# Issuing one tile's expert dot products and lookup table before the last tile pair, and computing one of three convolution blocks on ScalarE and GpSimd

## The chip, the cores and the metric

The kernel runs on one core of a Trainium2 chip. The metric is the device time of one execution in microseconds (us). The core's engines are named as the profile names them: PE is TensorE (PEld its weight loads), DVE is VectorE, ACT is ScalarE, POOL is GpSimd, SP is SyncE, which here issues the plain DMAs. Each engine works through its own queue of instructions in order and waits at an instruction whose inputs or buffers aren't ready.

## The reference: what is computed

One layer over 1024 tokens of width 1024, all in float32. Three parts matter here.

- **Token mixing.** A projection of the normalized input gives three groups of columns. The first (384 channels) goes through a gate and a causal depthwise convolution of width 31, then a layer norm over groups of 64 channels and a SiLU. The other two groups have a convolution of width 3 and a spatial gating. An output projection adds the result to the tokens.
- **Expert mixing.** For each token and each of 8 heads, two products with 128 keys are taken, the 16 best of each side and then the 16 best pairs: 128 experts out of 16384 per token, with softmax gates. Each chosen expert has a row of `expert_u` (dot product with the token, GELU, times the gate) and a row of `expert_v` (added with that weight).
- **Embedding gate.** A last projection, a sigmoid gate and a final normalization.

```python
y = causal_dwconv(y, conv_w) + conv_b          # width 31, 384 channels
ug = expert_u[ib]
act = jax.nn.gelu(jnp.einsum("td,tkd->tk", xb, ug)) * gb
vg = expert_v[ib]
return jnp.einsum("tk,tkd->td", act, vg)
```

## The kernel before: tiles, stages, queues

The 1024 tokens are 8 tiles of 128. The **front** works in four pairs of tiles, (0,1), (2,3), (4,5), (6,7), called the first to the fourth pair here. Each pair goes through `mix_in` (projection, convolutions, norms), `mix_out` (output projection) and `choose` (key products, the best 16, `select`).

In `mix_in` the convolution of width 31 has three blocks of 128 channels, j = 0, 1, 2, each with an accumulator `cacc` of 128x256 (128 channels by 256 tokens of the pair). Line 174 starts it on ACT. Lines 177 to 180 add 30 more taps to each block: 90 DVE instructions per pair, 360 in all, one every tap, each reading the shifted input `ya` and `cacc` and writing `cacc`. Lines 239 to 252 then norm each block; they take scratch tiles from the pool under the name `csq`, of which there are two.

The experts are done in two ways. Tiles 5, 6, 7 (`GATHER`) fetch the rows of each chosen expert by indirect DMA, which POOL issues (lines 536 and 566), and DVE forms the dot product (line 538) and the sum (line 568). Tiles 1 to 4 (`DENSE`) multiply with all 16384 experts on PE, with a weight table that holds the gate of each chosen expert and zero elsewhere. Tile 0 (`MIXED`) takes the dot products by gather and the second half by table.

A table is built by `gate_table` (lines 395 to 434): PE transposes gates and keys, ACT copies them to `gT`, `eT` and `mT`, of which there is one buffer each. Then 32 quads follow, each of four tokens: DVE compares the first key with a row of numbers (line 415), POOL does the second key in every other quad (line 421, four instructions), ACT in the remaining ones (lines 426 and 427), or DVE for the MIXED tile (line 423); PE multiplies (line 430), ACT copies out (line 431). Every eight quads SP stores the piece `st` to `Wd` (line 434). For the MIXED tile the gate is the finished weight `wm` (lines 541 to 547), so its table needs all 128 dot products per token, in four blocks of 32 (`u_step`).

Tables are issued by a **filler** list: `fill` (line 319) advances the first generator of the list by three steps at eight places in `mix_out` and eight in `choose`. Tables join the list after their pair's `choose`. The lines at the end of the front set it:

```python
    for t0, nt in ((0, 2), (2, 2), (4, 2), (6, 2)):
        yT = mix_in(t0, nt)
        choose(t0, nt, mix_out(t0, nt, yT))
        if t0 == UAT:
            for b in range(P // KB):
                u_step(MIXED, b, True)
        filler.extend(gate_table(t0 + t) for t in range(nt) if t0 + t in DENSE)
        if t0 == GAT:
            filler.append(gate_table(MIXED))
    while filler:
        fill()
```

With `UAT = GAT = 6` the MIXED tile's dot products and its table are written after the fourth pair. Then comes one block of dot products of tile 5 (line 640), and the front's buffers are released.

The order of the text isn't the order of the queues: the program is handed to a planner (`schedule_with_timeline_sim=True`, line 732) that simulates the engines and puts each instruction into its queue when it finds it ready, taking the one written earlier first. In an engine's queue the order is then fixed.

The front's gathers have three buffers `g`; the stage after it has five, in other space. That **dense stage** (lines 436 to 519) streams all experts: three products per matrix on PE (lines 481 to 483 and 504 to 506), splits on ACT and POOL (lines 468 to 477). Its buffers lie where the front's lay, and it needs every table. The gathers of tiles 5 to 7 (`experts`, line 550) run beside it. The **back** (lines 676 to 692) does the embedding gate of each tile.

Of the kernel before, what the change touches and what calls it, by code (L numbers as in the profile page):

```python
# [8 lines left out]
F32 = mybir.dt.float32  # L9
# [4 lines left out]
AF = mybir.ActivationFunctionType  # L14
OP = mybir.AluOpType
AX = mybir.AxisListType
P = 128
# [9 lines left out]
def trunk(ctx: ExitStack, tc: tile.TileContext, x, pT, w_inF, w_inV, chan, ln_c, w_sT, b_s, w_out, g_row,  # L27
          w_q, skT, expert_u, expert_uT, expert_v, w_pe, w_pg, out):
    nc = tc.nc
# [18 lines left out]
    ch = const.tile([P, chan.shape[1]], F32, name="ch")  # L48
# [7 lines left out]

    UAT, GAT, RATE = 6, 6, 3

    FG, BG = 3, 5

# [16 lines left out]
    work = fctx.enter_context(tc.tile_pool(name="work", bufs=2))  # L79
# [59 lines left out]
    def mix_in(t0, nt):  # L139

        T = nt * P
# [20 lines left out]
        yas, accs = [], []  # L162
# [13 lines left out]
            accs.append(acc)  # L176
        for k in range(1, 31):
            for j in range(3):
                nc.vector.scalar_tensor_tensor(accs[j], yas[j][:, k:k + T], ch[:, j * 31 + k:j * 31 + k + 1],
                                               accs[j], op0=OP.mult, op1=OP.add)  # L180


        for j in range(2):
# [3 lines left out]
            m = work.tile([P, 2 + T], F32, name="mb")  # L187
# [5 lines left out]
            for k in range(1, 3):  # L193
                nc.vector.scalar_tensor_tensor(acc, m[:, k:k + T], conv_b_w[:, j * 3 + k:j * 3 + k + 1], acc,
                                               op0=OP.mult, op1=OP.add)
# [432 lines left out]
# [9 lines that stand above are left out]
# [99 lines left out]
```

## Time and profile before

| | us |
|---|---|
| median of 3 runs (2860.47 to 2866.61) | 2861.89 |
| the profiled execution, its own time | 2862.61 |
| its span, first to last instruction | 2860.8 |
| PE busy (92% of the span) | 2620.5 |
| DVE busy (75%) | 2156.9 |
| POOL busy (68%) | 1945.5 |
| ACT busy (35%) | 1007.6 |

The mean granted PE clock of the profiled execution is 0.955 of full speed. Shares over the whole span mix the three stages, so the rows further down are taken stage by stage. A row's "idle" time is that of the engine just before the named instructions, with the instruction that ended it.

### The profile page before, as it was taken

To read this page: it belongs to the slowest core of one execution; us is meant where nothing else is said; L and a number is where in the kernel's file an instruction comes from. 1 tells how busy PE (TensorE), PEld (TensorE's weight loads), DVE (VectorE), ACT (ScalarE), POOL (GpSimd) and SP (SyncE) were. 2 spreads that over 40 slices of the span, in tenths; PEclk is the share of its full clock that TensorE was granted. 3 is DMA by queue.
4 is the path that set the end of the run, shared out by engine and by line. 5 is a ranking of instruction groups with operands and counts; after the bars stand their busy time and mean duration, and the time that the engine had idled before them with its cause. 6 is when DMAs were issued, how large, how long until landed. Compare 5 with 4: busy or idle time off the path is not lost.

```text
span 2860.8 us, 37645 instructions
## 1 busy us (share of the span) xinstructions
PE 2620.5 (92%) x12671; PEld 2203.2 (77%) x12671; DVE 2156.9 (75%) x4738; ACT 1007.6 (35%) x1930; POOL 1945.5 (68%) x1740
## 2 busy tenths in 40 slices
PE   7998999889678678999999999999999999999988
PEld 6887888688677656888787888878787788788767
DVE  5567888999977886777777777777777777677776
ACT  3312455335764544222322223232222322222342
POOL 0000377347876787888878888888887878888773
PEclk9998999899789779999999999999999999999999
DMA  6353688787657649899999999999999999999885
GB/s 203 129 185 120 236 300 301 242 304 253 221 206 274 228 184 339 317 324 344 331 333 328 331 347 330 338 329 342 325 336 329 328 348 332 335 339 324 299 290 174
DMA packets 299698, 820.92 MB, mean 287 GB/s; under 512 B 26096, under 2 KB 117616, under 8 KB 296944
## 3 DMA queue, kind: packets, MB, share of 16 engines
q0 software_dynamic: 129024, 469.82, 45.8%
q1 hardware_dynamic: 170480, 348.70, 35.6%
q8 instruction: 100, 1.64, 0.2%
q14 instruction: 94, 0.77, 0.1%
HBM read 764.93 MB, written 53.48 MB: 286 GB/s over the span
## 4 chain that ended last, share of the span: by engine, by line
PE 33%; DMA 23%; DVE 17%; POOL 13%; issue 10%; ACT 2%; SPq 0%; POOLq 0%; DVEq 0%; ACTq 0%
DMA g<-expert_u,idx 10%; DMA g<-expert_v,idx 10%; PE z L158 4%; DVE g L538 4%; POOL g L536 4%; PE mm L612 3%; POOL vl L477 3%; PE mm L504 3%; PE z L481 3%; PE z L482 3%; PE mm L505 3%; PE mm L506 3%; PE z L483 3%; PE mm L299 2%; PE mm L267 2%
## 5 line engine op out<-in xcount | busy, mean ns | idle before, releaser
L536 POOL DMA_INDIRECT g<-expert_u,idx x512 | 511.9, 1000 | 369.6 <-DVE g L538 163.2
L568 DVE SCALAR_TENSOR_TENSOR accP<-g,act,accP 128x1024 f32<-128x1024 f32 x384 | 493.2, 1284 | 210.9 <-DMA g<-expert_v,idx 207.4
L538 DVE SCALAR_TENSOR_TENSOR g<-g,nP 128x1024 f32<-128x1024 f32 x352 | 422.8, 1215 | 178.5 <-DMA g<-expert_u,idx 177.1
L566 POOL DMA_INDIRECT g<-expert_v,idx x384 | 367.7, 957 | 144.4 <-DVE accP L568 60.7
L504 PE MATMUL mm<-vh,ah 128*128 128x512 f32 x1024 | 400.3, 392 | 13.5 <-DVE accA L508 6.8
L481 PE MATMUL z<-nh,uh 128*128 128x512 f32 x1024 | 401.8, 393 | 8.1 <-DVE al L490 5.9
L482 PE MATMUL z<-nl,uh 128*128 128x512 f32 x1024 | 400.6, 391 | 2.0 <-DVE nl L446 2.0
L483 PE MATMUL z<-nh,ul 128*128 128x512 f32 x1024 | 400.2, 391 | 0.0
L505 PE MATMUL mm<-vl,ah 128*128 128x512 f32 x1024 | 399.2, 391 | 0.0
L506 PE MATMUL mm<-vh,al 128*128 128x512 f32 x1024 | 396.7, 390 | 0.0
L421 POOL TENSOR_SCALAR oh<-iota,eT,gT 128x128 f32<-128x128 f32 x320 | 314.5, 991 | 63.9 <-PE gt L430 50.8
L468 ACT CAST uh<-u 128x1024 fp32r<-128x1024 f32 x128 | 134.8, 1053 | 574.8 <-PE z L482 459.3
L477 POOL TENSOR_TENSOR vl<-v,vh 128x512 fp32r<-128x512 f32 x256 | 328.2, 1302 | 3.2 <-ACT vh L475 0.7
L470 POOL TENSOR_TENSOR ul<-u,uh 128x1024 fp32r<-128x1024 f32 x128 | 309.3, 2417 | 6.9 <-ACT uh L468 4.6
L430 PE MATMUL gt<-oh,oh 128*128 128x128 f32 x1280 | 221.4, 321 | 95.1 <-POOL oh L421 40.4
L430 PEld LDWEIGHTS gt<-oh,oh 128*128 128x128 f32 x1280 | 194.5, 224 | 123.1 <-POOL oh L421 82.6
L475 ACT CAST vh<-v 128x512 fp32r<-128x512 f32 x256 | 153.1, 621 | 306.9 <-DMA v<-expert_v 250.6
L538 DVE SCALAR_TENSOR_TENSOR g<-g,hrow 128x1024 f32<-128x1024 f32 x160 | 197.3, 1236 | 72.3 <-DMA g<-expert_u,idx 72.2
L158 PE MATMUL z<-aT,w 128*128 128x256 f32 x960 | 227.0, 393 | 16.0 <-DMA w<-w_inF 13.1
L299 PE MATMUL mm<-nT,w 128*128 128x256 f32 x1024 | 237.0, 383 | 4.4 <-DMA w<-w_q 4.4
L508 DVE TENSOR_TENSOR accA<-mm,accA 128x512 f32<-128x512 f32 x320 | 217.8, 684 | 27.0 <-PE mm L506 26.7
L504 PEld LDWEIGHTS mm<-vh,ah 128*128 128x128 f32 x1024 | 193.0, 189 | 56.7 <-DVE accA L508 9.8
(368 smaller groups left out, 4586.6 us busy)
## 6 DMA issues: line engine op xcount, KB each, us to landing
u<-expert_uT SPq DMA_DIRECT2D x128, 512.0 KB, 6.4
v<-expert_v SPq DMA_DIRECT2D x128, 512.0 KB, 4.9
Wd<-st SPq DMA_DIRECT2D x20, 2048.0 KB, 8.4
w<-w_q SPq DMA_DIRECT2D x64, 512.0 KB, 4.8
w<-Wd SPq DMA_DIRECT2D x128, 256.0 KB, 9.7
w<-w_inF SPq DMA_DIRECT2D x60, 512.0 KB, 3.6
wo<-w_out SPq DMA_DIRECT2D x32, 512.0 KB, 4.5
g<-expert_u,idx POOLq DMA_INDIRECT x512, 6.3
```

What stands on the lines that cost most here:

```text
L430: nc.tensor.matmul(pw[:, :, k], oh2[:, k], oh1[:, k], start=True, stop=True)
L477: nc.gpsimd.tensor_tensor(vl, v[:, s * 512:s * 512 + 512], vh.bitcast(F32), op=OP.subtract)
L481: nc.tensor.matmul(ph, uh[:, c], nh[:, c], start=c == 0, stop=False)
L482: nc.tensor.matmul(ph, uh[:, c], nl[:, c], start=False, stop=False)
L483: nc.tensor.matmul(ph, ul[:, c], nh[:, c], start=False, stop=c == 7)
L504: nc.tensor.matmul(po, ah[:, c], vh, start=i == 0, stop=False)
L505: nc.tensor.matmul(po, ah[:, c], vl, start=False, stop=False)
L506: nc.tensor.matmul(po, al[:, c], vh, start=False, stop=i == NG - 1)
L536: nc.gpsimd.indirect_dma_start(out=ug, out_offset=None, in_=expert_u, in_offset=bass.IndirectOffsetOnAxis(ap=idx[:, k:k + 1], axis=0))
L538: nc.vector.scalar_tensor_tensor(ug, ug, 1.0, ns[t, front], op0=OP.mult, op1=OP.mult, accum_out=dots[:, k - b * KB:k - b * KB + 1])
L566: nc.gpsimd.indirect_dma_start(out=vg, out_offset=None, in_=expert_v, in_offset=bass.IndirectOffsetOnAxis(ap=idx[:, kk:kk + 1], axis=0))
L568: nc.vector.scalar_tensor_tensor(acc, vg, act[:, k:k + 1], acc, op0=OP.mult, op1=OP.add)
```

## The change

Two edits, nothing else differs.

- `UAT` and `GAT` go from 6 to 4: the MIXED tile's four blocks of dot products are written behind the third pair, and its table joins the filler list behind that of tile 4, so that the list is worked off within the fourth pair's `mix_out` and `choose`.
- Of the three convolution blocks, block j = 2 loses its 30 DVE instructions per pair. In their place ACT multiplies the tap by its weight into a new scratch tile `csq` (the two that the norm uses too), and POOL adds it to `cacc`.

```diff
-    UAT, GAT, RATE = 6, 6, 3
+    UAT, GAT, RATE = 4, 4, 3
...
         for k in range(1, 31):
             for j in range(3):
-                nc.vector.scalar_tensor_tensor(accs[j], yas[j][:, k:k + T], ch[:, j * 31 + k:j * 31 + k + 1],
-                                               accs[j], op0=OP.mult, op1=OP.add)
+                tap, w = yas[j][:, k:k + T], ch[:, j * 31 + k:j * 31 + k + 1]
+                if j == 2:
+
+                    m = work.tile([P, T], F32, name="csq")
+                    nc.scalar.activation(m, tap, AF.Copy, scale=w)
+                    nc.gpsimd.tensor_tensor(accs[j], accs[j], m, op=OP.add)
+                else:
+                    nc.vector.scalar_tensor_tensor(accs[j], tap, w, accs[j], op0=OP.mult, op1=OP.add)
```

## Rows read from the trace of the kernel before

**Rows 1.** Stages: length; PE, PEld, DVE, ACT, POOL busy; clock; DMA share; GB/s.
```profile
0.00:286.00 286.00, 247.20 (x1386) 214.66 (x1386) 178.88 (x661) 82.49 (x183) 13.44 (x21) 0.97 0.48 159
286.00:787.00 501.00, 435.70 (x2589) 388.31 (x2590) 452.86 (x1531) 241.81 (x553) 294.29 (x273) 0.92 0.76 265
787.00:1042.00 255.00, 192.94 (x1067) 171.89 (x1065) 206.18 (x752) 152.03 (x358) 186.06 (x183) 0.81 0.60 217
1042.00:1085.00 43.00, 30.42 (x176) 25.51 (x176) 28.35 (x67) 13.36 (x25) 38.67 (x49) 0.87 0.69 263
1085.00:2727.00 1642.00, 1598.88 (x6948) 1309.29 (x6949) 1195.21 (x1632) 474.00 (x742) 1337.44 (x1130) 0.99 0.94 332
2727.00:2861.00 134.00, 115.41 (x510) 93.54 (x508) 95.44 (x100) 43.94 (x75) 75.61 (x87) 0.94 0.65 223
```

**Rows 2.** By line: count, ns min/median/max, first and last start in us.
```profile
L481 PE MATMUL z<-nh,uh x1024: 387/389/632, 1086.5 to 2689.2; 128*128 128x512 f32 x171
...
L508 DVE TENSOR_TENSOR accA<-mm,accA x320: 677/683/693, 1139.0 to 2727.5; 128x512 f32<-128x512 f32 x160
...
L571 ACT COPY hrow<-accP x3: 1016/1017/1017, 1702.3 to 2830.2; 128x1024 f32<-128x1024 f32 x3
```

**Rows 3.** By line, in the same columns: what ends just before the dense stage.
```profile
L434 SPq DMA_DIRECT2D Wd<-st x3: 319/319/320, 1059.3 to 1084.9; - x3
...
L530 ACT ACTIVATE nP<-hrow,rB x1: 1123/1123/1123, 1084.8 to 1084.8; 128x1024 f32<-128x1024 f32 x1
```

**Rows 4.** Timeline of PE: start us, us; the transposes that open the five tables.
```profile
304.06 0.27 PE L401 MATMUL gt<-ident,gate 128*128 128x128 f32 x1
...
627.00 0.27 PE L403 MATMUL gt<-ident,e 128*128 128x128 f32 x1
...
764.80 0.42 PE L401 MATMUL gt<-ident,gate 128*128 128x128 f32 x1
...
893.06 0.27 PE L401 MATMUL gt<-ident,gate 128*128 128x128 f32 x1
...
1016.52 0.42 PE L401 MATMUL gt<-ident,wm 128*128 128x128 f32 x1
```

**Rows 5.** Stretches between the tables, in the columns of the first group.
```profile
486.00:622.00 136.00, 116.17 (x665) 100.27 (x665) 122.14 (x416) 40.09 (x75) 45.59 (x44) 0.89 0.80 278
622.00:1016.00 394.00, 310.18 (x1779) 277.83 (x1778) 337.30 (x1260) 240.72 (x575) 292.90 (x275) 0.85 0.66 231
```

**Rows 6.** POOL's groups from 622 to 1085 us: busy, mean ns, idle before.
```profile
L421 POOL TENSOR_SCALAR oh<-iota,eT,gT 128x128 f32<-128x128 f32 x256 | 247.2, 975 | 58.8 <-PE gt L430 46.3 <-ACT eT L407 11.0
L536 POOL DMA_INDIRECT g<-expert_u,idx x79 | 91.1, 1153 | 55.2 <-DVE g L538 31.4 <-issue 5.0 <-DVE ti L334 4.2
```

**Rows 7.** The convolution on DVE: line 179 in 0 to 286, 286 to 787, 486 to 622, 622 to 1085 us.
```profile
L179 DVE SCALAR_TENSOR_TENSOR cacc<-ya,ch,cacc x180: 468/479/486, 31.5 to 182.1; 128x256 f32<-128x256 f32 x180
...
L179 DVE SCALAR_TENSOR_TENSOR cacc<-ya,ch,cacc x180: 455/472/718, 303.9 to 719.2; 128x256 f32<-128x256 f32 x180
...
L179 DVE SCALAR_TENSOR_TENSOR cacc<-ya,ch,cacc 128x256 f32<-128x256 f32 x48 | 21.7, 473 | 0.0
...
L179 DVE SCALAR_TENSOR_TENSOR cacc<-ya,ch,cacc 128x256 f32<-128x256 f32 x42 | 19.5, 475 | 0.0
```

**Rows 8.** The front's dot products and the MIXED tile's weights, by line.
```profile
L538 DVE SCALAR_TENSOR_TENSOR g<-g,hrow x160: 1154/1215/3060, 319.6 to 978.4; 128x1024 f32<-128x1024 f32 x160
...
L547 POOL TENSOR_TENSOR wm<-wm,gate x4: 269/402/602, 441.8 to 826.4; 128x32 f32<-128x32 f32 x4
```

**Rows 9.** Nearest prices: an ACT product, two POOL two-input operations, POOL's table instruction alone.
```profile
L192 ACT ACTIVATE bacc<-mb,ch x8: 503/504/507, 53.5 to 602.3; 128x256 f32<-128x256 f32 x8
...
L477 POOL TENSOR_TENSOR vl<-v,vh 128x512 fp32r<-128x512 f32 x256 | 328.2, 1302 | 3.2 <-ACT vh L475 0.7
...
L470 POOL TENSOR_TENSOR ul<-u,uh 128x1024 fp32r<-128x1024 f32 x126 | 303.6, 2410 | 6.9 <-ACT uh L468 4.6
...
L421 POOL TENSOR_SCALAR oh<-iota,eT,gT x64: 781/791/1460, 1018.6 to 1083.0; 128x128 f32<-128x128 f32 x64
```

## Prediction

> **What bounds the kernel now.** I read the stages first, because shares of the whole span mix three different limits. The busy time by stage [rows 1] cuts the run at 1085 us and 2727 us. From 1085 to 2727 the dense stage has PE busy 1599 of 1642 us at clock 0.99, with DMA at 0.94: nothing in the change touches its work, so it only starts sooner or later. Beside it run the gathers of tiles 5 to 7; dense ends with the last sum at 2727.5, the gathers with the copy at 2830.2 [rows 2]. Both begin with the same event, so a front that ends X earlier moves both by X, and the back with them.
>
> What ends the front? Just before PE's first dense product at 1086.5 [rows 2] stand the last store of a table piece at 1084.9 and, at 1084.8, the scaling of the token row from which the gather stage forms its dot products [rows 3]. Both wait for the MIXED tile's table. So I looked for what sets that table's end. The transposes that open the tables start at 304, 627, 765, 893 and 1016.5 us [rows 4]: the MIXED table is the last of a chain of four that runs without a gap from 627 to 1085, one behind the other since `gT`, `eT` and `mT` have one buffer. Its weights were ready at 826.4 [rows 8], so it waited 190 us for its turn and not for its inputs.
>
> What paces the chain? Tables 2, 3 and 4 took 138, 128 and 123 us (differences of the starts), the MIXED table, nearly alone, 69. From 622 to 1016 DVE is busy 337 of 394 us (86%), PE 79%, POOL 74% [rows 5]. POOL's queue shows why they couple: its 79 gathers there wait 31 us for DVE to free a gather buffer, and its table instructions 46 us for PE [rows 6]; behind a waiting gather stands the next quad. From 486 to 622 DVE is at 90% and POOL at 34% [rows 5]: no table runs there, as tile 2's choice isn't out of DVE yet. DVE is the engine nearest to full from 286 on (453 of 501 us, [rows 1]).
>
> **Part one, the convolution block: what DVE loses.** 360 instructions become 240. Of the 120 removed, 60 belong to the first two pairs (180 instructions end by 182 us, [rows 7]), where DVE is busy 179 of 286 us and PE 247 [rows 1]: worth nothing, PE sets the pace. The other 60 belong to the third and fourth pair. Their spacing is 0.46 us (19.5/42, 21.7/48, [rows 7]), so 60 x 0.46 = 27.6 us. Only 42 of those 180 lie behind 622 us, so 14 of the removed 60, 6.4 us, lie in the table chain and 46, 21.2 us, before it.
>
> What does the freed time before 622 do? The MIXED tile's dot products fill it: though written behind the fourth pair they run from 319.6 us on [rows 8], wherever DVE has room. One takes about 1.22 us of DVE (1.215 median), so some 17 of them move out of the chain's stretch, and 17 gathers with them. The chain's DVE load falls by 21.2 + 6.4 = 27.6 us, its POOL load by 17 x 1.153 = 20 us [rows 6]. With DVE pacing the chain, it ends 27.6 us earlier. Bounds: 0, if PE and POOL pace it, and 27.6/0.86 = 32 us, if DVE keeps its share. I take 27.6, one us for one.
>
> **What ACT and POOL gain.** 120 ACT products at 0.504 us [rows 9]: 60 us, 30 of them from 286 to 787 where ACT is busy 242 of 501 [rows 1]. Hidden; with no cover, 30 us. 120 POOL adds of 128x256: no such row, but 512 columns take 1.302 us and 1024 take 2.410 [rows 9], so 2.16 ns a column and 1.302 - 256 x 0.00216 = 0.75 us. Beside a busy DVE the table instruction takes 0.975 instead of 0.791 us on average [rows 6, 9], a factor 1.23, so 0.92 us. Bounds: 0.75 unstretched, and 1.4 at that instruction's longest over its median (1.460/0.791, [rows 9]). I take the mean stretch, 0.92. The first 60 meet a POOL that is busy 13 of 286 us [rows 1]. The third pair's 30 lie beside table 1, which has slack until table 2 starts at 627. Of the fourth pair's 30, about 14 fall behind 622: 14 x 0.92 = 13 us (20 at the upper bound), no more than the 20 us of gathers that leave. So POOL's load in the chain falls by 7 us; taken as nothing.
>
> The new waits: an ACT product needs one of two `csq` tiles and so the add two taps back. Behind a held product in ACT's queue stand the copies out of PSUM (lines 301, 308, 431), for which PE waits. I cost that at nothing in this sum, as POOL has 66% idle before 622, and price it in the second rival.
>
> **Part two, the move.** Nothing is added or removed. The 128 gathers, their 128 dot products, the row load, the four GELUs and gate products go ahead of the fourth pair in the planner's order. As they already fill gaps from 319.6 us on, only those left when the fourth pair's work is ready change place; the weights come earlier, where 190 us are spare. The table's 64 POOL instructions, 96 DVE and 128 PE instructions and four stores go ahead of most of the fourth pair's `choose`. On SP the key and query weights of `choose` then queue behind stores that wait for their piece; 16 of the 20 stores stand among such loads now, so I cost this at nothing. But the chain stays a chain: behind tile 4's table the MIXED one can't start sooner than now, and ahead of it the two only change places. I take 0. The other end is the stretch in which nothing but this table is left, 1042 to 1085: 43 us [rows 1], if it all went beside other work.
>
> **Sum.** Against the profiled execution's 2862.6 us (span 2860.8): 2862.6 - 27.6 - 0 = 2835.0. That execution stands 0.7 above the median shown, so 2834. What is late next: the same chain, 28 us earlier.
>
> **The rivals.** First, slower: **the adds stop DVE.** In place of the removed instruction POOL reads `cacc` and the product while DVE works on blocks 0 and 1, each of its instructions with two inputs from SBUF. If an add holds DVE for its length, 60 adds x 0.75 = 45 us in the third and fourth pair, against 27.6 saved: +17, so 2880. It decides from 27.6/0.75 = 37 holding adds on. For it: table instructions on POOL stretch from 0.791 to 0.975 us beside DVE, and a convolution step took up to 0.718 us with POOL busy, at most 0.486 with POOL idle [rows 6, 7, 9]. Against it: the median step is 0.472 us with POOL busy and 0.479 without [rows 7]. Held products on ACT would work the same way and sign. 0.25.
>
> The Trainium skill has a rule for this (SBUF — State Buffer, "Who interferes with whom"): a DVE instruction with two SBUF inputs and a GpSimd instruction that reads SBUF exclude each other for the whole instruction. By that rule the sum would be the 2880 of this rival; the trace agrees for POOL's stretch and hardly for DVE, whose median doesn't move, and no row has a two-input POOL operation beside the convolution.
>
> Second, **no change**: DVE's freed time only brings the MIXED weights sooner, which have 190 us spare, and the chain goes at the pace of PE and POOL (46 us of waits between them, [rows 6]); the planner leaves the table last. 2862. For it: POOL's 74% with waits both ways. Against: DVE at 86%. 0.13.
>
> Third, **both parts pay**: the MIXED table really goes beside the fourth pair's choice, and the 43 us fall away too: 2862.6 - 27.6 - 43 = 2792. Against it: DVE, PE and POOL are each at 73 to 81% from 787 to 1042 [rows 1], so there is little room for 69 us of coupled work. 0.10.
>
> **The numbers.** The forecast has 0.52; its own range is 2812 to 2854. A measurement of this kernel can tell 0.2%, 5.7 us, from no change. Faster: 0.52 + 0.10 = 0.62; same 0.13; slower 0.25. Cases of both signs are needed for 8 in 10: the range goes from the third rival's 2792 to the first's 2880.
>
> **What would show it.** Right: line 179 has 240 instructions of 0.47 us; the second table opens 15 to 25 us before 627; the MIXED table is still the last, right behind tile 4's, and opens near 990; the first dense product comes near 1058; the length from there to the end stays 1774 us. Wrong: convolution steps or dot products on DVE that lengthen, or ACT products that wait for POOL (first rival); table starts that don't move (second); a MIXED table that ends before the last choice is out of DVE, with PE going straight from choice to dense (third). A dense stage that itself changes length would be none of these.

## The result and the profile after

The changed kernel is slower: 2906.3 us median against 2861.2 for the kernel before on the same chip, ratio 1.0151 (95% interval 1.0128 to 1.0174). The profiled execution took 2905.06 us (2862.61 before), so 42.5 us more. The forecast was 2834.

First the stages of the changed kernel, by busy time in stretches; the columns are those of [rows 1], and the cuts are the same up to 1085 us.

```profile
0.00:286.00 286.00, 248.93 (x1366) 215.15 (x1366) 154.40 (x541) 100.29 (x223) 64.27 (x80) 0.96 0.47 158
286.00:787.00 501.00, 423.26 (x2439) 373.27 (x2438) 427.74 (x1354) 250.04 (x574) 322.81 (x311) 0.90 0.72 252
787.00:1042.00 255.00, 187.84 (x1123) 171.92 (x1124) 200.92 (x761) 160.00 (x377) 178.58 (x181) 0.84 0.65 229
...
1127.00:2762.00 1635.00, 1593.61 (x6924) 1302.19 (x6925) 1195.78 (x1630) 467.53 (x729) 1333.83 (x1124) 0.99 0.94 332
```

The dense stage, to its last sum at 2762, has its work and nearly its length (1635 against 1642 us), only later. In the front, from 286 to 787, POOL is busy 29 us more and ACT 8 us; DVE (428 against 453) and PE (423 against 436) are less busy: the front is slower although the two engines with the most to do got emptier.

Next, by line: the two ends of the front that answer to [rows 2] and [rows 3], and PE's transposes that open tables 2 to 5, which answer to [rows 4].

```profile
L440 SPq DMA_DIRECT2D Wd<-st x3: 320/320/326, 1089.4 to 1125.7; - x3
...
L487 PEld LDWEIGHTS z<-nh,uh x1024: 186/188/334, 1127.3 to 2731.6; 128*128 128x128 f32 x171
...
L577 ACT COPY hrow<-accP x3: 1017/1018/1019, 1745.0 to 2870.0; 128x1024 f32<-128x1024 f32 x3
```
```profile
645.55 0.33 PE L409 MATMUL gt<-ident,e 128*128 128x128 f32 x1 [1.28 <-DVE e L384]
...
794.23 0.27 PE L407 MATMUL gt<-ident,gate 128*128 128x128 f32 x1
...
921.87 0.27 PE L407 MATMUL gt<-ident,gate 128*128 128x128 f32 x1
...
1049.46 0.42 PE L407 MATMUL gt<-ident,wm 128*128 128x128 f32 x1
```

The last table store comes at 1125.7 us instead of 1084.9, the dense stage starts right behind it, and the last copy of the gather stage comes at 2870.0 instead of 2830.2. From the first dense instruction to the end of the span it is 1776 us, 1774 before. So all of the loss arises in the front, as all of the gain was meant to. The second table opens at 645.6 instead of 627.0, the third at 794 instead of 765, the fourth at 922 instead of 893, the last at 1049.5 instead of 1016.5. So 19 us of the loss build up before the chain of tables and 11 in its first link, none in the second; the last 12 us come behind the fourth table's opening, where no convolution runs any more, and what makes these isn't shown.

The convolution's three instructions, by line (count, ns min/median/max, first and last start), and ACT's waits:

```profile
L184 POOL TENSOR_TENSOR cacc<-cacc,csq x120: 712/738/6079, 46.7 to 669.2; 128x256 f32<-128x256 f32 x120
...
L186 DVE SCALAR_TENSOR_TENSOR cacc<-ya,ch,cacc x240: 459/480/1536, 32.1 to 721.6; 128x256 f32<-128x256 f32 x120
...
L183 ACT ACTIVATE csq<-ya,ch x120: 491/508/535, 46.1 to 666.7; 128x256 f32<-128x256 f32 x120
its engine sat idle before it (us, times) until:
  POOL cacc L184: 81.3, 74
```

DVE's convolution steps, at most 718 ns before [rows 7], now take up to 1536; ACT's products wait 81 us for POOL's adds. Both are signs that the prediction had listed for its first rival. An add takes 0.74 us in the median and 6.08 at the longest; that longest one is taken up below.

### The profile page after: what moved, and what is told of

Read it like the earlier page. It is cut to its first block, busy times and chain, and to the rows that moved or that the text cites. A ratio compares the mean times of both kernels' runs of the same rounds, so it can differ in the third digit from the quotient of the medians.

```text
span 2903.3 us, 37904 instructions
## 1 busy us (share of the span) xinstructions
PE 2630.7 (91%) x12671; PEld 2208.0 (76%) x12671; DVE 2146.7 (74%) x4618; ACT 1063.2 (37%) x2053; POOL 2043.2 (70%) x1860
## 4 chain that ended last, share of the span: by engine, by line
PE 34%; DMA 19%; DVE 18%; POOL 14%; issue 11%; ACT 2%; POOLq 0%; SPq 0%; DVEq 0%; ACTq 0%
DMA g<-expert_u,idx 9%; DMA g<-expert_v,idx 8%; POOL g L542 4%; DVE g L544 4%; PE mm L510 4%; PE mm L511 4%; PE mm L512 4%; PE z L487 4%; PE z L488 4%; PE z L489 3%; PE mm L618 3%; DVE accP L574 3%; POOL oh L427 3%; POOL vl L483 3%; PE z L158 2%
## 5 line engine op out<-in xcount | busy, mean ns | idle before, releaser
L158 PE MATMUL z<-aT,w 128*128 128x256 f32 x960 | 234.5, 402 | 23.7 <-DVE mb L195 10.3
L487 PEld LDWEIGHTS z<-nh,uh 128*128 128x128 f32 x1024 | 193.8, 189 | 56.1 <-DVE al L496 10.9
```

The lines of the kernel that those rows point to most:

```text
L487: nc.tensor.matmul(ph, uh[:, c], nh[:, c], start=c == 0, stop=False)
```

## The experiments

All ratios are to the kernel before on the same chip. "DVE" is DVE's busy time in the profiled execution; before it is 2156.9 us. Runs e5 to e7, e9, e13 to e16 and e18 leave out or replace part of the convolution, as their text says.

| run | ratio | 95% interval | DVE, us |
|---|---|---|---|
| the change | 1.0151 | 1.0128 to 1.0174 | 2146.7 |
| e1 the move alone | 1.0030 | 1.0012 to 1.0048 | 2159.8 |
| e2 the convolution edit alone | 1.0169 | 1.0144 to 1.0194 | 2150.5 |
| e3 e2 with four product tiles | 1.0135 | 1.0113 to 1.0156 | 2150.4 |
| e4 e2 in the first two pairs | 1.0051 | 1.0029 to 1.0073 | 2147.5 |
| e12 e2 in the last two pairs | 1.0122 | 1.0107 to 1.0138 | 2167.1 |
| e5 products, no adds | 0.9976 | 0.9960 to 0.9992 | 2111.9 |
| e6 adds, no products | 1.0157 | 1.0123 to 1.0191 | 2154.3 |
| e7 neither | 0.9991 | 0.9972 to 1.0010 | 2113.6 |
| e8 blocks in another order | 1.0000 | 0.9985 to 1.0015 | 2157.2 |
| e9 two fills for each add | 1.0065 | 1.0041 to 1.0089 | 2113.0 |
| e14 three fills | 1.0027 | 1.0011 to 1.0043 | 2114.4 |
| e13 three fills, last two pairs | 1.0001 | 0.9985 to 1.0017 | 2138.1 |
| e15 one-input POOL instruction | 1.0072 | 1.0044 to 1.0099 | 2120.4 |
| e16 adds on block 0, no products | 1.0023 | 1.0004 to 1.0041 | 2145.9 |
| e18 adds on block 1, no products | 1.0085 | 1.0066 to 1.0104 | 2157.9 |
| e17 e2 on block 0 | 1.0102 | 1.0079 to 1.0125 | 2147.0 |
| e10 table quads from POOL to DVE | 0.9986 | 0.9970 to 1.0003 | 2205.5 |
| e11 e2 and e10 | 1.0168 | 1.0141 to 1.0194 | 2191.4 |

### Which edit, and which pairs

```diff
# e1
-    UAT, GAT, RATE = 6, 6, 3
+    UAT, GAT, RATE = 4, 4, 3
# e2: the second hunk of the change without the first; in e4 and e12 its condition is
-                if j == 2:
+                if j == 2 and t0 < 4:
# (t0 >= 4 in e12)
```

> Only the MIXED tile's dot products and table are moved (UAT = GAT = 4); the convolution stays on DVE. Theory H (ACT products that wait for POOL's adds hold ACT's queue): no loss, 2855 to 2870 us. Theory M (the dot products, now ahead of the fourth pair, delay its mixing on DVE): most of the 45 us, above 2885.

> Only the convolution's third block goes to ACT and POOL; UAT = GAT = 6 as before. H and theory P (the adds fill POOL's queue and so slow the tables and gathers): most of the loss, 2890 to 2915. M: about 2861. The forecast's reason (DVE is relieved): 2835.

The move alone costs 0.3%, hardly more than can be told from nothing. In its profiled execution tables 2 to 5 open at 623.3, 771.4, 898.8 and 1015.9 us and the dense stage starts at 1087.1, 0.6 us from where it did: the front's length is the same, so the move's 0 stands where the prediction placed it. That execution is the fastest of the ten, 11 us under their median, so it doesn't show where the 0.3% lie. The convolution edit alone is as slow as the whole change.

> The convolution edit in the first two pairs alone, where POOL has hardly any other work; 60 of the 120 adds. H and P: a small loss, from the first two mixes ending 5 to 10 us later, 2862 to 2872. If a mere change of the planner's order is what costs: any value, as large as with all four pairs.

> The convolution part of the change in the third and fourth pairs alone; the first two pairs as before. With the first two pairs alone the ratio was 1.0051, with all four 1.0169: if the two halves simply add, 1.010 to 1.014 here. The first mix ends at 110 us as before.

The two halves add: 0.51% and 1.22% make 1.73%, measured 1.69%. A third of the loss comes from the first two pairs, which the prediction held to be worth nothing.

### Which instruction of the edit

```diff
# e3, against e2: four tiles in turn instead of two
-                    m = work.tile([P, T], F32, name="csq")
+                    m = work.tile([P, T], F32, name="csq" if k % 2 else "xc")
# e5, against e2: the adds left out
-                    nc.gpsimd.tensor_tensor(accs[j], accs[j], m, op=OP.add)
# e6, against e2: the tap itself is added, unscaled, with no product on ACT
-                    m = work.tile([P, T], F32, name="csq")
-                    nc.scalar.activation(m, tap, AF.Copy, scale=w)
-                    nc.gpsimd.tensor_tensor(accs[j], accs[j], m, op=OP.add)
+                    nc.gpsimd.tensor_tensor(accs[j], accs[j], tap, op=OP.add)
# e7, against e6: block 2 keeps its first tap alone
-                    nc.gpsimd.tensor_tensor(accs[j], accs[j], tap, op=OP.add)
+                    pass
# e8, against the kernel before
-            for j in range(3):
+            for j in (2, 1, 0):
```

> As the convolution alone, but the products alternate between the tiles csq and xc, so that four buffers stand between ACT and POOL instead of two. H: at least half of the convolution's loss comes back and ACT's waits for the adds (81 us in the changed kernel) fall below 40. P: no more than a quarter of the loss comes back, as the adds are the same.

> UAT = GAT = 6. Block j = 2 keeps its 120 ACT products, and the 120 POOL adds are left out, so this block's convolution is incomplete. Theory H (products that wait for POOL's adds, one queue holding the other): the loss is gone, at or below the kernel before, ratio 0.985 to 1.002. Theory A (ACT's own 60 us of products are the cost): ratio 1.010 or more. Theory P (POOL's adds as work): ratio 0.985 to 1.002.

> UAT = GAT = 6. Block j = 2 has the 120 POOL adds, of the unscaled input, and no ACT products, so its convolution is unweighted. H: ratio 0.985 to 1.004, as no ACT instruction waits for POOL in the convolution. P: most of the loss stays, 1.010 to 1.017. A: 0.985 to 1.002.

> UAT = GAT = 6. Block j = 2 keeps only its first tap: 120 DVE instructions are gone and nothing stands in their place. The forecast's own term: 27.6 us less, ratio 0.990. If DVE's freed time is only filled by other waits: 0.998 to 1.002. If a mere change of the planner's order costs tens of us: above 1.005.

> The kernel before with the three blocks' taps written in the order 2, 1, 0 in place of 0, 1, 2: the same instructions, another tie for the planner. If the result hangs on how the planner happens to fall: a ratio off 1 by more than 0.005. Under H and P: 0.998 to 1.002.

Two things follow. **The forecast's own term isn't there.** e7 has 120 fewer DVE instructions and nothing in their place; DVE is busy 43 us less (2156.9 to 2113.6), and the time stays the same within 0.3%. **The adds carry the loss.** With them and without products it is 1.57%; with products and without them there is none (0.24% less time). So products held behind adds aren't needed for the loss. Four tiles cut ACT's waits from 84 to 63 us, not below 40 as held products would have it, and gave back a fifth, so e3 by itself decides little. The other order of e8 is as fast as the first.

What the adds do to DVE shows in the last column of the table: e6 has the DVE instructions of e7 and is busy 40.7 us longer, 0.34 us for each of 120 adds.

### The adds or POOL's time

An add could hurt in two ways: P, POOL and DVE shut each other out; or Q, POOL's queue is simply longer, so that gathers and table quads come later. Fills write the same accumulator and read nothing.

```diff
# e9, against e6; e14 has range(3); e13 has range(3) and "if j == 2 and t0 >= 4"
-                    nc.gpsimd.tensor_tensor(accs[j], accs[j], tap, op=OP.add)
+                    for _ in range(2):
+                        nc.gpsimd.memset(accs[j], 0.0)
# e15, against e6
-                    nc.gpsimd.tensor_tensor(accs[j], accs[j], tap, op=OP.add)
+                    nc.gpsimd.tensor_scalar(accs[j][:, 0:P], accs[j][:, 0:P], w, w, op0=OP.mult, op1=OP.add)
```

> Block 2 of the convolution keeps only its first tap (that part of the computation is left out), and each of its 120 steps gives POOL two fills of the 128x256 accumulator, which write SBUF and read none of it. One fill of 128x128 took 0.20 us at the start of the kernel before, so some 0.7 us for a step, beside 0.80 us for an add without a product: POOL's queue is as full as with the adds. Theory P (an add on POOL and a DVE instruction with both inputs in SBUF shut each other out, and the loss is DVE's): DVE's convolution instructions stay under 0.5 us, the first mix ends at 110 us as before, the ratio lies within 0.997 to 1.002. Theory Q (POOL's time itself: gathers and one-hots queue behind the adds): the first mix ends at 110 us too, since POOL has nothing else to do there, but the second table opens at 640 to 655 us instead of 629, and the ratio is 1.008 to 1.013.

> As the run with two fills for each of block 2's 120 steps in all four pairs (block 2 keeps only its first tap), with three: 360 fills of 0.31 us are 113 us of POOL, more than the 96 us of the adds without products. Theory P (the loss is DVE and POOL shutting each other out): 0.997 to 1.004, so that the 1.0065 of the two fills was the order in which the planner laid out that program. Theory Q (POOL's time itself): half as much again as with two, 1.009 to 1.013.

> Each of block 2's 120 steps is one POOL instruction with a single SBUF tensor as input, a 128x128 half of the accumulator times a tap plus a tap (block 2's convolution is replaced by this). The one-hots of that form and size take 0.79 us when alone, so 95 us of POOL, as much as the adds. If reading SBUF on POOL at all shuts out DVE's instructions with two SBUF inputs: 17 convolution instructions ahead of the first mb take 10 us or more (6.8 with fills, 12.7 with adds), first mix at 114 to 119 us, ratio 1.008 to 1.018. If it takes two inputs on POOL as well: 6.8 us, first mix at 110, ratio 0.998 to 1.005.

The first pair shows the mechanism by itself, since POOL has no gathers and no table there. Below are the timelines (start, us, instruction, count, idle time) of DVE and POOL in e6, with adds: 17 convolution steps, the product `mb` for which PE waits, and POOL's run beside them.

```profile
46.28 12.69 DVE L184 SCALAR_TENSOR_TENSOR cacc<-ya,ch,cacc 128x256 f32<-128x256 f32 x17
58.89 0.41 DVE L193 TENSOR_TENSOR mb<-z,sg 128x256 f32<-128x256 f32 x1
...
73.22 0.42 DVE L193 TENSOR_TENSOR mb<-z,sg 128x256 f32<-128x256 f32 x1 [0.55 <-ACT sg L190]
...
47.19 24.67 POOL L182 TENSOR_TENSOR cacc<-cacc,ya 128x256 f32<-128x256 f32 x30 [15.35 <-DVE cacc L184]
```

The same in e14, with three fills for each add; DVE's queue has the same 17 steps there:

```profile
46.12 6.81 DVE L185 SCALAR_TENSOR_TENSOR cacc<-ya,ch,cacc 128x256 f32<-128x256 f32 x17
52.92 0.42 DVE L194 TENSOR_TENSOR mb<-z,sg 128x256 f32<-128x256 f32 x1
...
63.42 0.42 DVE L194 TENSOR_TENSOR mb<-z,sg 128x256 f32<-128x256 f32 x1 [1.43 <-ACT sg L191]
...
47.01 30.91 POOL L183 MEMSET cacc<- 128x256 f32 x84 [15.45 <-ACT cacc L174]
```

And in e15, with one SBUF tensor as POOL's input:

```profile
44.48 6.81 DVE L184 SCALAR_TENSOR_TENSOR cacc<-ya,ch,cacc 128x256 f32<-128x256 f32 x17
51.20 0.42 DVE L193 TENSOR_TENSOR mb<-z,sg 128x256 f32<-128x256 f32 x1
...
45.42 23.83 POOL L182 TENSOR_SCALAR cacc<-cacc,ch 128x128 f32<-128x128 f32 x30 [15.06 <-ACT cacc L174]
...
45.42 6.19 POOL L182 TENSOR_SCALAR cacc<-cacc,ch 128x128 f32<-128x128 f32 x1 [15.06 <-ACT cacc L174]
```

The last line is the first of the thirty by itself.

Seventeen steps take 12.69 us beside adds (0.75 each) and 6.81 (0.40 each) beside fills, with POOL busy throughout in both. e15's 6.81 has another reason: there DVE shut POOL out, as the times say. POOL's first instruction started inside the seventeen steps, took 6.19 us and ended 0.3 us behind the last of them; the median of all 120 is 0.45. It isn't the price of the first instruction of its kind either: the first of the kernel before (line 421) takes 2.15 us. So e15 doesn't show that POOL instructions with one SBUF input leave DVE alone; it shows the other side of the same exclusion.

`mb`, one of whose inputs is in PSUM, takes 0.41 to 0.42 us in all three. PE can't go on without `mb`: over the run its projections (line 158 in all these kernels) wait 12.6 us for it in e6, 10.3 in the change and not at all in e14. The second `mb` starts at 73.2 us with adds and at 63.4 with fills. In the kernel before it starts at 63.3, so fewer steps ahead of it bring nothing: with fills DVE sits idle 1.43 us before it, for ACT. That is how relief can be worth nothing and delay its full length. The first pair ends 10 us late in the change (last SiLU at 119.4 us instead of 109.6), 9 us in e6 (118.3), and 1 to 2 us in e14 and e15 (111.2 and 110.8), as in e7 (111.0), which has nothing in place of the steps.

The change itself comes to its 10 us by a longer way than e6. This is its first pair, first POOL, then DVE, then ACT, and DVE's next eleven steps:

```profile
46.71 6.08 POOL L184 TENSOR_TENSOR cacc<-cacc,csq 128x256 f32<-128x256 f32 x1 [15.43 <-ACT csq L183]
...
45.39 6.81 DVE L186 SCALAR_TENSOR_TENSOR cacc<-ya,ch,cacc 128x256 f32<-128x256 f32 x17
56.84 0.42 DVE L195 TENSOR_TENSOR mb<-z,sg 128x256 f32<-128x256 f32 x1 [4.63 <-ACT sg L192]
...
52.82 0.51 ACT L183 ACTIVATE csq<-ya,ch 128x256 f32<-128x256 f32 x1 [5.79 <-POOL cacc L184]
...
62.49 8.30 DVE L186 SCALAR_TENSOR_TENSOR cacc<-ya,ch,cacc 128x256 f32<-128x256 f32 x11
```

Here the seventeen steps keep their 0.40 us and the first add is the one that waits: it takes 6.08 us and ends 0.6 us behind the last step. ACT's third product waits 5.79 us for it, the copy `sg`, which `mb` needs, stands in ACT's queue behind products, and DVE sits idle 4.63 us. Only then do adds and steps alternate, and the next eleven steps take 8.30 us (0.75 each; 5.68 for the same eleven in e14). In e6 the first add, in the same place, took 0.85 us and slowed DVE from there on. The 6.08 aren't a cost of the first add as such: in e3 and e4, with the same products, it took 0.94 and 0.93 us, and e4, where adds and steps alternate from the start, ends the first pair just as late (last SiLU at 119.4 us). So POOL and DVE shut each other out in both, but the one that waits differs, and in the change a part of the delay reaches DVE through ACT. How the loss of the change divides between these two ways, no run shows.

For the third and fourth pair e12 and e13 are the comparison: adds, with their products on ACT, and fills of the same POOL time.

> In the third and fourth pairs block 2 keeps only its first tap (that part is left out) and each step gives POOL three fills of the accumulator instead of an add: 180 fills of 0.31 us are 56 us of POOL, as much as the 56 us that the 60 adds of these pairs took in the changed kernel, and none of it reads SBUF. Theory Q (in these pairs POOL's time itself is the cost): 21 us for the 38 us of fills of the run before make 32 us for 56, ratio 1.009 to 1.013, the same as with the adds within 0.3%. Theory P (the shutting out is the cost here as in the first pair): the fills cost 1.002 to 1.007, well under the adds.

Busy time by stretch, in the columns of [rows 1], then two DVE groups from 340 to 650 us (count, busy, mean ns, idle before). With adds (e12):

```profile
340.00:490.00 150.00, 128.21 (x724) 111.49 (x724) 120.90 (x325) 83.74 (x217) 132.38 (x126) 0.92 0.75 268
490.00:650.00 160.00, 131.24 (x746) 115.26 (x744) 142.95 (x444) 61.46 (x126) 84.09 (x81) 0.90 0.74 258
...
L544 DVE SCALAR_TENSOR_TENSOR g<-g,hrow 128x1024 f32<-128x1024 f32 x73 | 94.5, 1296 | 23.8 <-DMA g<-expert_u,idx 23.7
L186 DVE SCALAR_TENSOR_TENSOR cacc<-ya,ch,cacc 128x256 f32<-128x256 f32 x74 | 46.9, 649 | 0.1
```

With fills (e13):

```profile
340.00:490.00 150.00, 130.50 (x765) 114.48 (x764) 114.40 (x334) 79.55 (x208) 129.24 (x185) 0.95 0.78 274
490.00:650.00 160.00, 144.98 (x859) 128.90 (x858) 144.43 (x511) 55.77 (x112) 95.31 (x156) 0.96 0.85 293
...
L543 DVE SCALAR_TENSOR_TENSOR g<-g,hrow 128x1024 f32<-128x1024 f32 x80 | 98.3, 1231 | 39.5 <-DMA g<-expert_u,idx 39.3
L185 DVE SCALAR_TENSOR_TENSOR cacc<-ya,ch,cacc 128x256 f32<-128x256 f32 x84 | 39.1, 480 | 0.1
```

POOL is as full from 340 to 490 in both (132 and 129 us). DVE's steps take 0.65 us with adds and 0.48 with fills, the dot products 1.30 and 1.23; from 490 to 650 DVE is as busy with adds for 67 instructions fewer, and PE gets 14 us less done (at a granted clock of 0.90 instead of 0.96). DVE's busy time over the run differs by 29 us, the times by 1.2%, 34.6 us. e6 and e14 compare the same without products, over all four pairs: POOL is busy 2050.0 and 2061.0 us, DVE 2154.3 and 2114.4, and the losses are 1.57 and 0.27%. Nor is it the wait for the last POOL instruction of a block: in the third pair the last fill of e14 ends at 520 us and the last add of e6 at 481, and yet the pair's last SiLU starts at 558 in e14 and at 579 in e6. So POOL's time as such (Q) isn't the cost here; what adds and DVE's steps do to each other (P) is. That the longer steps are what makes these two pairs late is argued from these rows; only the first pair shows it step by step.

One part doesn't fit. Fills in all pairs cost 0.65% with two and 0.27% with three, and e15 0.72%, with at most 2 us of delay in the first pair and 0, 1 and 7 us more of DVE's busy time than e7. More POOL time costing less isn't Q. These programs also differ in the order into which the planner put the queues, and that may move a run by about half a per cent; no run shows this by itself (e8's other order cost nothing).

### Where the adds stand, and a lighter POOL

```diff
# e16 (against e6: adds of unscaled taps) and e17 (against e2); e18 is e16 with j == 1
-                if j == 2:
+                if j == 0:
# e10 (against the kernel before) and e11 (against e2): POOL builds every fourth quad, DVE the next odd one
-                    if n_gt[0] % 2:
+                    if n_gt[0] % 4 == 1:
...
-                    elif t == MIXED:
+                    elif n_gt[0] % 2 or t == MIXED:
```

> The adds without products on block 0 instead of block 2 (block 0's taps are added unscaled), so that the planner lays out another order with the same adds. If the loss is the adds' own, whatever the order: first mix 6 to 10 us late, ratio 1.012 to 1.018. If it was one unlucky order: 0.998 to 1.008.

> Adds without products on block 1, whose samples are ready between those of block 0 (1.0023) and block 2 (1.0157). If the place in the pair sets the cost: between the two, 1.005 to 1.012, first mix at 116 to 119 us. If it is the luck of each order: anywhere from 1.000 to 1.016, with no relation to the place.

> The convolution part of the change, whole, on block 0 in place of block 2. Block 0's samples are ready first, so the adds run earlier in each pair. If the place of the adds is what costs, as the 1.0023 of adds without products on block 0 says: 0.999 to 1.006, and better than the change itself by at least 1%. If the adds cost the same wherever they stand, and the run on block 0 was one lucky order: 1.012 to 1.018.

The same 120 adds cost 0.23, 0.85 and 1.57% on blocks 0, 1 and 2, though DVE's busy time rises by 32, 44 and 41 us over e7. The first pair ends 6 us late in e16 and 8 in e18 (last SiLU at 116.0 and 118.0 us); for e16 that is as much as the whole loss (0.23%, 6.6 us). In the third pair the adds stand in POOL's timeline like this in e16, on block 0:

```profile
307.86 11.91 POOL L182 TENSOR_TENSOR cacc<-cacc,ya 128x256 f32<-128x256 f32 x13 [7.30 <-ACT cacc L174]
322.43 1.37 POOL L540 DMA_INDIRECT g<-expert_u,idx  x1 [2.66 <-DVE idx L396]
...
326.93 6.66 POOL L182 TENSOR_TENSOR cacc<-cacc,ya 128x256 f32<-128x256 f32 x5
333.74 1.90 POOL L540 DMA_INDIRECT g<-expert_u,idx  x1
```

Thirteen run before the first gather of the pair. In e6, on block 2, the first of them starts at 361.9 us and the 30th at 480. So the loss goes with the place in the pair, in the order that e18's expectation gave. But the whole change on block 0 came out at 1.0102, not at the 0.999 to 1.006 expected of it: there the products add 0.8%, on block 2 they added nothing. Place and laid-out order can't be told apart further with these runs.

> The kernel before with every second of POOL's groups of four one-hots (40 groups) built on DVE, in the way that the MIXED tile's already are (128x128, 0.40 us each on DVE against 0.98 us on POOL): POOL gives up 157 us between 345 and 1085 us and DVE takes 64 us. Theory Q (POOL's queue sets the pace of the third and fourth pairs): tables open earlier from the second on, the last table store comes 15 to 40 us earlier, ratio 0.985 to 0.995. Theory P (DVE sets the pace, and the adds hurt by slowing it): DVE's further 64 us come on top, ratio 1.005 to 1.02.

> The convolution part of the change (products on ACT, adds on POOL) together with the half of POOL's one-hot groups moved to DVE. POOL gets about 96 us of adds and gives up 157 us. Theory Q: most of the loss of the convolution part (ratio 1.017 alone) goes, ratio 0.990 to 1.003, and what stays is the first pair's 9 us. Theory P: DVE has more to do beside the same adds, ratio 1.017 or more.

Both theories were wrong on e10. DVE got 49 us more to do and POOL 146 us less (1799.3 against 1945.5 busy), and the time moved by 0.14%, with no change inside the interval. It isn't DVE's load as such, then: 49 us more cost nothing here, in the tables and with POOL relieved at the same places, and 41 us cost 1.57% in e6, where they fall on the convolution. That the place makes this difference is argued, not shown. Together with e7, no relief of either engine by itself shortens the front; this is the nearest to a version that beats the kernel before, beside e5, which computes less. With the adds beside it (e11) the loss is whole again, though POOL has less to do than before: one more sign against Q.

## Why the prediction was wrong

- **The step that failed** is "With DVE pacing the chain, it ends 27.6 us earlier". e7 takes those instructions away, DVE is busy 43 us less, and the time shows 0 (0.9991), the lower bound that the text named ("0, if PE and POOL pace it"). DVE's high share was read as a limit; e10 shows that 49 us more on DVE, with POOL lighter, cost nothing either.
- **The second failed term** is POOL's load "taken as nothing". It was reckoned as POOL's busy time only. The add itself was sized well: 0.92 us foretold, 0.90 on average in the change (107.8/120). e13 confirms the rest of that part: POOL time without reads costs nothing in these pairs. The cost is what an add and DVE's steps do to each other.
- **"Worth nothing, PE sets the pace"** for the first two pairs is right for relief and wrong for delay: 0.51% (e4).
- **The first rival had the engines, the mechanism and the sign.** Its price was wrong twice. It took 0.75 us of DVE for each add; DVE's busy time rose by 0.34 us for each (e6 against e7). It set 27.6 us saved against that, and nothing is saved. And it counted 60 adds, where all 120 cost. Its 2880 was 26 us short. The point from which it decides (37 adds, to pay back the saving) doesn't exist without a saving.
- The evidence against it, a median step of 0.472 us beside a busy POOL [rows 7], came from POOL instructions with one tensor as input. In e15 such an instruction stood still for 6.19 us while DVE's steps kept their 0.40, so steps that don't lengthen don't show that the engines leave each other alone. The rows could not show what a two-input instruction does, and the text said so; it still gave that row weight.
- The Trainium skill's rule (SBUF — State Buffer, "Who interferes with whom") was the better guide for the sign. These runs agree with it for the two-input adds, and for fills, which it excepts since they only write SBUF. For an instruction on POOL that reads one SBUF tensor e15 agrees as well, only that POOL was the engine that waited (6.19 us against a median of 0.45).
- **ACT's products** were costed at nothing on ACT: e5 shows that. Their waits (81 us) were costed at nothing too, and listed with the first rival; in the change's first pair they hold DVE for 4.63 us. e6 has no products and the same loss, so the loss doesn't need them.
- **The move** was given 0: in e1's profiled execution the front keeps its length, and the whole is 0.1 to 0.5% slower. The MIXED table stays the last of the chain, as foretold, and the dense-to-end length stayed at 1776 us (foretold 1774).
- **Still open**: why the adds cost 0.2% on one block and 1.6% on another with about as much more of DVE's busy time, what decides which of the two engines waits, how the change's loss divides between DVE's longer steps and ACT's held queue, and what e9's and e15's 0.7% are made of.

## What to carry to other kernels

Before two-input work is moved from VectorE to GpSimd, look for VectorE instructions with two SBUF inputs beside it: here each removed step freed 0.36 us of VectorE (43.3/120) and each add took 0.34 back. Look at the longest instructions of both engines, not at one engine's median: where VectorE's steps don't lengthen, GpSimd may be the one that stands still. An engine at 86% is a bound only if taking work away shortens the stage; a version that just leaves the work out tells that in one run, before anything is built to take its place. Where a planner orders the queues, try the same work at another place of the loop before judging it.

## What the runs showed of the hardware

- Beside each other, adds on POOL and convolution steps on DVE slow down: a 128x256 add takes 0.62 us at least and 0.82 beside the steps (24.67/30, e6), a step 0.75 instead of 0.40. That is less than one behind the other in full (0.62 + 0.40).
- The hold can be one-sided, to either side. In e6 the first add took 0.85 us and the seventeen steps 0.75 each; in the change the add in that place took 6.08 us, until seventeen steps of 0.40 were through. e15's one-input instruction takes 0.45 us in the median, and its first one 6.19 in the same way; beside the later ones eleven steps take 0.59 us each (6.46/11), against 0.52 beside fills (5.68/11). By line, in the columns used above, and e6's first add and the eleven steps of e15 and e14:

```profile
L182 POOL TENSOR_SCALAR cacc<-cacc,ch x120: 437/450/6187, 45.4 to 625.4; 128x128 f32<-128x128 f32 x120
...
47.19 0.85 POOL L182 TENSOR_TENSOR cacc<-cacc,ya 128x256 f32<-128x256 f32 x1 [15.35 <-DVE cacc L184]
...
54.65 6.46 DVE L184 SCALAR_TENSOR_TENSOR cacc<-ya,ch,cacc 128x256 f32<-128x256 f32 x11
...
56.31 5.68 DVE L185 SCALAR_TENSOR_TENSOR cacc<-ya,ch,cacc 128x256 f32<-128x256 f32 x11
```

- A fill of 128x256 on POOL takes 0.31 us, half an add, and doesn't slow DVE's steps, nor is it slowed by them (301 to 341 ns over all 240 in e9).
